# Norm powers on ScalarE and the causal mask before the exponential in a one-core hybrid decoder layer

## The chip, the cores and the metric

The kernel runs on one core of a Trainium2 chip, in one launch. The metric is the device time in microseconds. The median of three runs is 2675.95 us (2674.31 to 2677.8). Engine names are those of the profile: PE is TensorE, PEld its weight loads, DVE is VectorE, ACT is ScalarE, POOL is GpSimd and SP is SyncE.

## The reference

One layer over 512 tokens of width 2048, in float32. The parts that the change touches are the norms of queries and keys and the attention without softmax:

```python
proj = rmsnorm(x, attn_norm_g[i]) @ w_in[i]       # u, v_sgu, q, k, v_att, g_a, g_b
q = rmsnorm(q.reshape(B, S, SB_HEADS, SB_HEAD_DIM), q_norm_g[i])   # 8 heads of 128
k = rmsnorm(k.reshape(B, S, SB_HEADS, SB_HEAD_DIM), k_norm_g[i])
# for each block of 128 queries:
z = jnp.einsum('bhqd,bhkd->bhqk', qi, kf) * scale
strict = key_pos[None, :] < q_pos[:, None]
log_beta = jax.nn.log_sigmoid(z)
log_1m = jnp.where(strict, jax.nn.log_sigmoid(-z), 0)
tail = lax.cumsum(log_1m, axis=3, reverse=True) - log_1m
w = jnp.where(strict, jnp.exp(log_beta + tail), 0)
out = jnp.einsum('bhqk,bhkd->bhqd', w, vf)
```

Around it stand a gated chunk mixing of 8 groups (`y_a`), `x += (sigmoid(g_a) * (y_a @ w_up_a) + sigmoid(g_b) * (y_b @ w_up_b)) @ w_o`, a SwiGLU of hidden width 5632, and a last gate `x += sigmoid(rmsnorm(x) @ w_pg) * (p @ w_ple)`.

## The kernel before

All tensors are held transposed: features on the 128 partitions, the 512 tokens along the free dimension. Each float32 operand is split into a high part, rounded by ScalarE (`whi`, `parts`), and a low remainder, formed by VectorE (`wlo`). Most products are Strassen products on 2 x 2 blocks (lines 284 to 286 and 695), with the sums mixed on VectorE and ScalarE (lines 718 to 799).

Weights come in units through `Weights`: SyncE loads the blocks (L329, L331), GpSimd issues one more load that adds onto what has landed (L351), ScalarE rounds (L347), VectorE sums (L363) and subtracts (L344). Units are prepared a few ahead (`prepare_early`, `prepare_late`) with three slots.

The order is made while the program is laid out. The projections run in four rounds: q, k and v for two heads each, then three or four gate projections. TensorE's stream is the sequence of weight units. After each unit or part of one, `tick` advances a counter and lets the waiting side steps run; such a step is a generator started with `beside`, which says by `yield n` after how many ticks it goes on. The side steps of a round are `q_prep`, `k_prep`, `v_prep` and `attention`, so their small matmuls stand among the large ones of the next projections. A scheduler orders each engine's instructions within these bounds, and each engine works through its queue in that order.

In `q_prep` and `k_prep` a head is transposed into a PSUM bank of the two-buffer tag `small` (`flip`, L1032). `token_rms` squares and sums it on ScalarE (L1039), adds a scaled epsilon on VectorE (L1047) and raises to the power -0.5 on GpSimd (L1049). For q VectorE multiplies by 128^-0.5 (L1064). ScalarE scales the transposed q by the result (`times`, L1054), and the same line scales v by the first norm. k's result scales the logits later (L1109, L1110).

`attention` runs over 2 heads x 4 key blocks = 8 blocks a round, 32 in all, each in four steps. `stage_a` makes logits and log(1 + exp(-|z|)) on ScalarE. `stage_m` forms two tensors on VectorE: `w`, the log of beta (L1116), and `s`, the negated log of 1 - beta (L1118); GpSimd masks `s` (L1120), copies a row (L1127) and clears row 0 (L1128). `stage_b` and `stage_c` split `s` (L1131, L1135). `stage_d` sums `s` over keys with a triangular matmul (L1141, L1142), subtracts it from `w` on VectorE (L1146), takes the exponential on ScalarE (L1147) and masks on GpSimd (L1148). `stage_m` of the next block is laid out in the tick before `stage_d` of the present one. `finish` multiplies the four `w` with v (L1157).

Operands of later products are `Form` objects. Those with spilled inputs stand in the list `builds`; `tick` fetches the block of one that has none (`fetch`) and later starts its steps. `plain` is called by a product that needs a form's plain half at once and advances its steps there; if the form has no block, its first step loads one itself (`raw`).

Of the kernel before, what the change touches and what calls it, by code (L numbers as in the profile page):

```python
# [12 lines left out]
F32 = mybir.dt.float32  # L13
F32R = mybir.dt.float32r
AF = mybir.ActivationFunctionType
ALU = mybir.AluOpType
# [3 lines left out]
P = 128  # L20
T = 512
NT = T // P
# [5 lines left out]
GROUPS = 8  # L28
PLE = 256
EPS = 1e-6  # L30

OUT = "SSSSPPPP"
PASSES = "SSSSSSSS", "SSSSSSSS", "SSSSPP"
# [34 lines left out]
def hybrid_layer(  # L68
# [18 lines left out]
    nc = tc.nc  # L87

    consts = ctx.enter_context(tc.tile_pool(name="consts", bufs=1))
# [99 lines left out]
    builds, seconds = deque(), deque()  # L189
# [243 lines left out]
    class Form(Staged):  # L433
# [36 lines left out]
        def plain(self):  # L470

            if self.kind == "P":
                return self.get()
            while not self.at_plain:
                self.advance()
            self.go_on()
            return self.halves(self.operand())
# [422 lines left out]
    def load_x():  # L900
# [18 lines left out]
                            fill=0.0, base=0, channel_multiplier=1)  # L919
# [3 lines left out]
    expo = consts.tile([P, 8], F32, name="expo")  # L923
# [67 lines left out]
    norm1 = Norm()  # L991
# [32 lines left out]
        return att[tag].f(start, start + n)  # L1024

    eps_cols = consts.tile([P, NT], F32, name="eps_cols")

    def flip(o):

# [10 lines left out]
                                 accum_out=ms[:, t : t + 1])  # L1040
        return ms

    def token_rms(ps, r):

        norm1.row()
        ms = squares(ps)
        nc.vector.scalar_tensor_tensor(out=ms, in0=ms, scalar=1.0 / P, in1=eps_cols,  # L1047
                                       op0=ALU.mult, op1=ALU.add)
        nc.gpsimd.tensor_tensor(out=r, in0=ms, in1=expo[:, :NT], op=ALU.pow)  # L1049

    def times(dst, ps, r):
        for t in range(NT):
# [3 lines left out]
    def q_prep(o, i):  # L1056


        for h in range(2):
            yield 2  # L1060
            ps = flip(o[:, h * T : (h + 1) * T])
            q, r = take(T), rms_tile()[:, :NT]
            token_rms(ps, r)
            nc.vector.tensor_scalar(out=r, in0=r, scalar1=float(P) ** -0.5, scalar2=None,  # L1064
                                    op0=ALU.mult)
            yield 1
            times(q.f(), ps, r)
            yield 2
            if not h:
                y_b[i] = take(1024)  # L1070
            nc.scalar.activation(y_b[i].f(h * T, (h + 1) * T), flip(q.f()), AF.Copy,
                                 scale=gcol[:, g_q : g_q + 1])
            give(q)
# [12 lines left out]
    def attention(rnd, kT, rk, v):  # L1086
        state = {}
        yield 1
        qT = y_b[rnd].f()
        zh, zl = (att[t].own() for t in ("zh", "zl"))  # L1090

        def sums(j):
            return a_tile("zs", (NT - j) * P, j % 2 * T)

        def weights(h, j):
            return a_tile(f"w{j}", (NT - j) * P, (j == NT - 1) * h * P)

        def first(j):

            return (sums(j) if j == NT - 1 else a_tile("first", (NT - j) * P, (j == 1) * 2 * P))[0:1]  # L1100

        def stage_a(h, j):
            n = (NT - j) * P
            r = rk[:, 4 * h + j : 4 * h + j + 1]
            z = small_bank()[:, :n]
            c = h * T + j * P
            nc.tensor.matmul(z, kT[:, c : c + P], qT[:, c : (h + 1) * T], start=True, stop=True)  # L1107
            l, s = a_tile("l")[:, :n], sums(j)
            nc.scalar.activation(l, z, AF.Abs, scale=r)  # L1109
            nc.scalar.activation(s, z, AF.Copy, scale=r)  # L1110
            nc.scalar.activation(l, l, AF.Exp, scale=-1.0)
            nc.scalar.activation(l, l, AF.Ln, bias=1.0)

        def stage_m(h, j):
            l, s, w = a_tile("l")[:, : (NT - j) * P], sums(j), weights(h, j)
            nc.vector.scalar_tensor_tensor(out=w, in0=s, scalar=0.0, in1=l,  # L1116
                                           op0=ALU.min, op1=ALU.subtract)
            nc.vector.scalar_tensor_tensor(out=s, in0=s, scalar=0.0, in1=l,  # L1118
                                           op0=ALU.max, op1=ALU.add)
            nc.gpsimd.affine_select(out=s[:, :P], in_=s[:, :P], pattern=[[1, P]],  # L1120
                                    compare_op=ALU.is_gt, fill=0.0, base=0,
                                    channel_multiplier=-1)


            if j < NT - 1:
                if j:
                    nc.gpsimd.tensor_copy(first(j), s[0:1])  # L1127
                nc.gpsimd.memset(s[0:1, :P], 0.0)  # L1128

        def stage_b(j):  # L1130
            nc.scalar.activation(zh[:, : (NT - j) * P], sums(j), AF.Copy)  # L1131

        def stage_c(j):
            n = (NT - j) * P
            in_turn(nc.vector.tensor_tensor(out=zl[:, :n], in0=sums(j), in1=att["zh"].f(0, n),  # L1135
                                            op=ALU.subtract))

        def stage_d(h, j):
            n, w = (NT - j) * P, weights(h, j)
            tp, t = small_bank()[:, :n], tris[j < NT - 1]  # L1140
            nc.tensor.matmul(tp, t, zh[:, :n], start=True, stop=False)  # L1141
            nc.tensor.matmul(tp, t, zl[:, :n], start=False, stop=True)  # L1142
            if j:
                nc.vector.tensor_tensor(out=sums(j - 1)[0:1, P:], in0=tp[0:1], in1=first(j),
                                        op=ALU.add)
            nc.vector.tensor_tensor(out=w, in0=w, in1=tp, op=ALU.subtract)  # L1146
            nc.scalar.activation(w, w, AF.Exp)  # L1147
            nc.gpsimd.affine_select(out=w[:, :P], in_=w[:, :P], pattern=[[1, P]],  # L1148
                                    compare_op=ALU.is_gt, fill=0.0, base=0,
                                    channel_multiplier=-1)  # L1150
            state[h, "w", j] = w

        def finish(h):
            y = small_bank()
            for j in range(NT):
                c = h * T + j * P
                nc.tensor.matmul(y[:, j * P :], v[:, c : c + P], state.pop((h, "w", j)),  # L1157
                                 start=j == 0, stop=j == NT - 1)
            nc.scalar.activation(qT[:, h * T : (h + 1) * T], y, AF.Copy)
            if h == 1:  # L1160
                nc.sync.dma_start(out=y_spill[rnd], in_=qT)
                give(y_b[rnd])
                y_done["b", rnd] = True

        blocks = [(h, j) for h in range(2) for j in range(NT - 1, -1, -1)]
        stage_a(*blocks[0])
        yield 1
        stage_m(*blocks[0])
        yield 1
        stage_a(*blocks[1])  # L1170
        for i, (h, j) in enumerate(blocks):
            ahead = blocks[i + 1 : i + 3]
            stage_b(j)
            yield 1
            if i == NT:
                finish(0)
            stage_c(j)
            if ahead:
                stage_m(*ahead[0])
            yield 1  # L1180
            stage_d(h, j)
            if ahead[1:]:
                stage_a(*ahead[1])
            yield 1
        yield 1
        finish(1)
        if rnd == 3:
            for tag in ("first", "k", "v", "zs", "zh", "zl"):
                give(att.pop(tag))
# [109 lines left out]
    for n, ((w, i), pr) in enumerate(zip(order, made())):  # L1299
        if n == 0:  # L1300
            row1 = norm1.row()
            nc.vector.tensor_scalar(out=eps_cols, in0=norm1.mean, scalar1=EPS, scalar2=None,
                                    op0=ALU.mult)
        if n == 0:
            a_tiles()
        o = pr.out(block(w, i) if n < 3 else None)
        if w == "q":
            beside(q_prep(o, i))
        elif w == "k":
            kT, rk = o, rms_tile()  # L1310
            beside(k_prep(kT, rk))
            beside(attention(i, kT, rk, a_tile("v", 1024)), 6)
        elif w == "v":
            beside(v_prep(o, a_tile("v", 1024)))
        elif w == "s":
            scaled(o, row1)
            nc.scalar.activation(o, o, AF.Gelu_apprx_tanh)
            beside(sgu_v(i, o))
        elif w == "u":
            scaled(o, row1)  # L1320
            nc.scalar.activation(o, o, AF.Gelu_apprx_tanh)
            nc.vector.tensor_tensor(out=y_a[i].f(), in0=o, in1=y_a[i].f(), op=ALU.mult)
            y_done["a", i] = True
        else:
            d = tc.dram_tile([P, 1024], F32, name=nm("gsp"))
            nc.sync.dma_start(out=d, in_=o)
            gate_spill[w, i] = d
# [96 lines left out]
    for c, units in enumerate(hs):  # L1424
# [3 lines left out]
        for j in range(KU):  # L1428
# [8 lines left out]
            if not end:  # L1437
                after(2, lambda o=o, j=j: nc.gpsimd.dma_start(
                    out=spill["x1", j], in_=o, accum_op=ALU.add))
# [123 lines left out]
```

## Time and profile before

| | |
|---|---|
| median of three runs | 2675.95 us (2674.31 to 2677.8) |
| the profiled execution | 2676.21 us |
| its span, first to last instruction | 2674.5 us |
| granted TensorE clock, mean | 0.999 |
| the four attention rounds lie at | about 100 to 600 us |

The profile is of one execution. A row of a group gives line, engine, operation, shapes and count, then busy time and mean duration in ns, then the idle time just before these instructions and what ended it. A row of the waits gives who waited for whom, the total in us, how often, and the longest. In the timeline the first two numbers are start and duration in us.

### The profile page before, as it was taken

Reading aid. Unit: us, or ns where it says so; the run is one execution under the profiler, and the core shown is the slowest. Engines: PE = TensorE matmul, PEld = TensorE weight load, DVE = VectorE, ACT = ScalarE, POOL = GpSimd, SP = SyncE. Lnnn points to the kernel's source line nnn. Section 1 sums busy time; section 2 is a strip of 40 time slices with the busy share of each in tenths; the row PEclk is TensorE's granted clock in tenths of the full one; section 3 lists DMA queues with packets and bytes.
Section 4 is the critical chain, followed back from the end, with each engine's and each line's share of the span. In section 5 each row is a group of like instructions: output and inputs, shape, how many; then the busy total and the mean of one; then the engine's idle time right before and its main releaser. Section 6 shows DMA issues by size and latency. Waiting matters only on the chain.

```text
span 2674.5 us, 42586 instructions
## 1 busy us (share of the span) xinstructions
PE 2647.8 (99%) x15496; PEld 2322.1 (87%) x15496; DVE 2206.1 (82%) x3720; ACT 1392.0 (52%) x2171; POOL 471.2 (18%) x565
## 2 busy tenths in 40 slices
PE   8999999999999999999999999999999999999999
PEld 7889898988998889988888888888888888889898
DVE  8587878787887666678888888888889989989776
ACT  7656565665554334365444444444445445445543
POOL 0232323232220000001111111111111211211010
PEclk9999999999999999999999999999999999999999
DMA  7577777777776457668888888888788989978784
GB/s 230 151 186 175 180 173 184 173 179 201 178 187 199 141 154 210 188 213 195 220 217 206 207 202 201 204 202 206 195 208 226 263 219 272 226 238 257 242 241 132
DMA packets 285939, 540.25 MB, mean 202 GB/s; under 512 B 25632, under 2 KB 138016, under 8 KB 285728
## 3 DMA queue, kind: packets, MB, share of 16 engines
q1 hardware_dynamic: 224624, 424.25, 49.0%
q0 software_dynamic: 61104, 113.27, 27.0%
q8 instruction: 121, 1.98, 0.3%
q14 instruction: 90, 0.74, 0.1%
HBM read 490.24 MB, written 47.19 MB: 201 GB/s over the span
## 4 chain that ended last, share of the span: by engine, by line
PE 89%; DVE 5%; ACT 2%; DMA 2%; issue 1%; POOL 1%; SPq 0%; DVEq 0%; ACTq 0%; POOLq 0%
PE ps L695 48%; PE ps L286 11%; PE ps L285 11%; PE ps L284 11%; PE small L695 6%; DVE wlo L344 1%; DVE out L754 1%; PE small L1157 1%; DMA wholes<-x 1%; PE small L1032 1%; DVE wholes L363 1%; ACT whi L347 1%; DVE parts L275 0%; PE small L1107 0%; POOL wholes L1120 0%
## 5 line engine op out<-in xcount | busy, mean ns | idle before, releaser
L695 PE MATMUL ps<-parts,whi 128*128 128x512 f32 x3960 | 1324.8, 397 | 0.3 <-DVE p L754 0.3
L347 ACT ACTIVATE whi<-wholes 128x512 fp32r<-128x512 f32 (+3 forms) x933 | 866.5, 942 | 785.1 <-DVE wholes L363 270.9
L344 DVE TENSOR_TENSOR wlo<-wholes,whi 128x512 fp32r<-128x512 f32 (+3 forms) x933 | 974.4, 1078 | 82.5 <-ACT whi L347 82.1
L695 PEld LDWEIGHTS ps<-parts,wlo 128*128 128x128 f32 x3960 | 743.7, 188 | 167.8 <-issue 1.0
L695 PE MATMUL ps<-parts,wlo 128*128 128x256 f32 x3960 | 784.3, 279 | 0.1
L285 PE MATMUL ps<-parts,whi 128*128 128x256 f32 (+1 forms) x2070 | 678.3, 328 | 1.0 <-DVE parts L275 0.9
L286 PE MATMUL ps<-parts,wlo 128*128 128x256 f32 (+1 forms) x2070 | 677.9, 328 | 1.1 <-DVE wlo L344 1.1
L284 PE MATMUL ps<-parts,whi 128*128 128x256 f32 (+1 forms) x2048 | 668.0, 328 | 8.2 <-ACT parts L274 5.9
L695 PEld LDWEIGHTS ps<-parts,whi 128*128 128x128 f32 x3960 | 637.7, 189 | 6.1 <-issue 1.0
L285 PEld LDWEIGHTS ps<-parts,whi 128*128 128x128 f32 x2070 | 392.5, 190 | 41.4 <-DVE parts L275 2.5
L284 PEld LDWEIGHTS ps<-parts,whi 128*128 128x128 f32 x2048 | 388.2, 190 | 44.0 <-ACT parts L274 7.4
L286 PEld LDWEIGHTS ps<-parts,wlo 128*128 128x128 f32 x2070 | 392.8, 190 | 35.5 <-DVE wlo L344 2.3
L363 DVE TENSOR_TENSOR wholes<-wholes 128x256 f32<-128x256 f32 (+1 forms) x806 | 338.7, 420 | 21.3 <-DVE wlo L344 3.0
L754 DVE TENSOR_TENSOR out<-out,ps 128x256 f32<-128x256 f32 x460 | 190.5, 416 | 142.1 <-ACT out L751 141.8
L351 POOL DMA_DIRECT2D wholes<-w_ffn_in x172 | 150.1, 872 | 690.0 <-DVE wholes L363 268.5
L351 POOL DMA_DIRECT2D wholes<-w_in x132 | 117.8, 894 | 480.6 <-DVE wholes L363 125.9
L695 PE MATMUL small<-parts,whi 128*128 128x512 f32 x440 | 174.5, 397 | 0.0
L275 DVE TENSOR_TENSOR parts<-wholes,parts 128x1024 fp32r<-128x1024 f32 (+4 forms) x138 | 131.5, 965 | 18.9 <-ACT parts L274 18.9
L274 ACT ACTIVATE parts<-wholes 128x1024 fp32r<-128x1024 f32 (+4 forms) x138 | 113.2, 845 | 44.8 <-DVE wholes L513 25.7
L351 POOL DMA_DIRECT2D wholes<-w_ffn_out x64 | 55.9, 873 | 355.2 <-DMA wholes<-w_ffn_out 87.6
L751 ACT ACTIVATE out<-ps 128x256 f32<-128x256 f32 x243 | 91.0, 384 | 46.6 <-PE ps L695 43.3
L1403 ACT ACTIVATE out<-out 128x512 f32<-128x512 f32 x44 | 27.9, 633 | 159.6 <-DVE out L1402 159.6
(120 smaller groups left out, 1735.5 us busy)
## 6 DMA issues: line engine op xcount, KB each, us to landing
wholes<-w_ffn_in SPq DMA_DIRECT2D x172, 384.0 KB, 5.7
wholes<-w_in SPq DMA_DIRECT2D x132, 384.0 KB, 4.8
wholes<-w_ffn_in SPq DMA_DIRECT2D x172, 256.0 KB, 4.9
wholes<-w_ffn_in POOLq DMA_DIRECT2D x172, 256.0 KB, 5.4
wholes<-w_in SPq DMA_DIRECT2D x132, 256.0 KB, 4.1
wholes<-w_in POOLq DMA_DIRECT2D x132, 256.0 KB, 4.9
wholes<-w_ffn_out SPq DMA_DIRECT2D x64, 384.0 KB, 6.2
wholes<-hid SPq DMA_DIRECT2D x42, 512.0 KB, 6.1
```

What stands on the lines that cost most here:

```text
L274: return (nc.scalar.activation(hi, src, AF.Copy), nc.vector.tensor_tensor(out=lo, in0=src, in1=hi.bitcast(F32), op=ALU.subtract))
L275: nc.vector.tensor_tensor(out=lo, in0=src, in1=hi.bitcast(F32), op=ALU.subtract))
L284: nc.tensor.matmul(ps, sh, mh, start=start, stop=False)
L285: nc.tensor.matmul(ps, sh, ml, start=False, stop=False)
L286: return nc.tensor.matmul(ps, sl, mh, start=False, stop=stop)
L344: in_turn(nc.vector.tensor_tensor(out=self.lo[:, blocks], in0=r, in1=h.bitcast(F32), op=ALU.subtract))
L347: in_turn(nc.scalar.activation(h, r, AF.Copy))
L351: nc.gpsimd.dma_start(out=raw[:, 3:5], in_=self.src[:, 1:3], accum_op=ALU.add)
L363: in_turn(nc.vector.tensor_tensor(out=o, in0=x, in1=y, op=ALU.add))
L695: m = nc.tensor.matmul(out, l, r, start=first and k == 0, stop=last and k == 1)
L751: in_turn(nc.scalar.activation(out, x, AF.Copy, scale=scale))
L754: in_turn(nc.vector.tensor_tensor(out=out, in0=x, in1=y, op=op))
```

## The change

`token_rms` takes a scale and an epsilon tile, and its power becomes two ScalarE activations, Ln and then Exp with scale -0.5. For q it is called with scale 1 and an epsilon times 128, so that the factor 128^-0.5 is in the result and the VectorE rescaling goes. The mask on `w` moves from `stage_d`, after the exponential with fill 0, to the end of `stage_m`, ahead of it, with fill -10000. `plain` takes a form out of `builds` before it advances its steps.

```diff
+MASKED = -1e4
...
             if self.kind == "P":
                 return self.get()
+            if not self.at_plain and self in builds:
+                builds.remove(self)
             while not self.at_plain:
                 self.advance()
...
+    eps_q = consts.tile([P, NT], F32, name="eps_q")
...
-    def token_rms(ps, r):
+    def token_rms(ps, r, scale=1.0 / P, eps=eps_cols):
 
         norm1.row()
         ms = squares(ps)
-        nc.vector.scalar_tensor_tensor(out=ms, in0=ms, scalar=1.0 / P, in1=eps_cols,
+        nc.vector.scalar_tensor_tensor(out=ms, in0=ms, scalar=scale, in1=eps,
                                        op0=ALU.mult, op1=ALU.add)
-        nc.gpsimd.tensor_tensor(out=r, in0=ms, in1=expo[:, :NT], op=ALU.pow)
+        nc.scalar.activation(ms, ms, AF.Ln)
+        nc.scalar.activation(r, ms, AF.Exp, scale=-0.5)
...
             q, r = take(T), rms_tile()[:, :NT]
-            token_rms(ps, r)
-            nc.vector.tensor_scalar(out=r, in0=r, scalar1=float(P) ** -0.5, scalar2=None,
-                                    op0=ALU.mult)
+            token_rms(ps, r, 1.0, eps_q)
...
                 nc.gpsimd.memset(s[0:1, :P], 0.0)
+            nc.gpsimd.affine_select(out=w[:, :P], in_=w[:, :P], pattern=[[1, P]],
+                                    compare_op=ALU.is_gt, fill=MASKED, base=0,
+                                    channel_multiplier=-1)
...
             nc.scalar.activation(w, w, AF.Exp)
-            nc.gpsimd.affine_select(out=w[:, :P], in_=w[:, :P], pattern=[[1, P]],
-                                    compare_op=ALU.is_gt, fill=0.0, base=0,
-                                    channel_multiplier=-1)
...
-            nc.vector.tensor_scalar(out=eps_cols, in0=norm1.mean, scalar1=EPS, scalar2=None,
-                                    op0=ALU.mult)
+            for eps, c in ((eps_cols, EPS), (eps_q, EPS * P)):
+                nc.vector.tensor_scalar(out=eps, in0=norm1.mean, scalar1=c, scalar2=None,
+                                        op0=ALU.mult)
```

## The prediction

> **What bounds the kernel now.** I read the page first: busy time by engine and the chain that ended last.
>
> ```profile
> span 2674.5 us, 42586 instructions
> ...
> PE 2647.8 (99%) x15496; PEld 2322.1 (87%) x15496; DVE 2206.1 (82%) x3720; ACT 1392.0 (52%) x2171; POOL 471.2 (18%) x565
> ...
> PE 89%; DVE 5%; ACT 2%; DMA 2%; issue 1%; POOL 1%; SPq 0%; DVEq 0%; ACTq 0%; POOLq 0%
> ```
>
> TensorE has work in 2647.8 of 2674.5 us, so all its idle time is 26.7 us, 1.0%. The edit neither adds nor removes a matmul. It can pay only where it takes away a wait of TensorE (or a low clock), and it can cost only by making new ones. So the second view is who TensorE waited for (total us, times, longest).
>
> ```profile
> PE small L1142 <- DVE parts L1135: 3.5, 4, 0.9
> PE small L1032 <- ACT wholes L1054: 2.2, 1, 2.2
> PE small L1157 <- POOL wholes L1148: 2.2, 4, 0.6
> ...
> PE small L1214 <- ACT wholes L1054: 1.3, 1, 1.3
> ...
> PE small L1107 <- ACT wholes L1054: 0.7, 3, 0.2
> ```
>
> The list names the places. L1148 is the mask after the exponential, which moves: 2.2 us, four times, once per round. The 2.2 us at L1032 is a transpose waiting for L1054, the scaling by the norms' powers, in round 0. L1214 is the gating branch, whose power (L931) stays on GpSimd; the rows left out belong to the start, the weights and later stages. Third, the granted clock: read in windows of 100 us it is 1.00 everywhere but in one, so I cut that one more finely around the 2.2 us wait (time, PE, PEld, DVE, ACT, POOL busy, PEclk, DMA).
>
> ```profile
> 100.00:200.00 100.00, 95.88 (x581) 83.06 (x580) 78.58 (x148) 63.18 (x133) 35.34 (x46) 0.98 0.70 173
> ```
>
> ```profile
> 100.80:104.20 3.40, 1.06 (x8) 0.83 (x9) 2.77 (x6) 2.61 (x11) 1.64 (x2) 1.00 0.59 86
> 104.20:107.60 3.40, 3.40 (x17) 3.21 (x16) 0.33 (x1) 2.37 (x7) 1.21 (x2) 0.50 0.58 183
> ```
>
> Behind the stretch in which TensorE had 1.06 us of work in 3.40 stands one stretch of 3.40 us at clock 0.50. The wait thus had a second price: half of 3.40, 1.70 us.
>
> **Part 1: the powers of q and k go to ScalarE.** Sixteen GpSimd powers and eight VectorE rescalings go; 32 tiny ScalarE instructions (Ln, Exp on 128x4) come.
>
> ```profile
> L1039 ACT ACTIVATE sq<-small 128x128 f32<-128x128 f32 x96 | 26.5, 278 | 13.8 <-PE small L1032 11.9
> ...
> L1049 POOL TENSOR_TENSOR rr<-ms,expo 128x4 f32<-128x4 f32 x16 | 24.6, 1540 | 3.3 <-DVE ms L1047 3.3
> ...
> L1039 ACT ACTIVATION_READ_ACCUMULATOR sq<-small 128x1 f32 x96 | 19.0, 198 | 0.0
> ...
> L1064 DVE TENSOR_SCALAR rr<-rr 128x4 f32<-128x4 f32 x8 | 1.4, 170 | 12.7 <-POOL rr L1049 12.7
> ```
>
> ```profile
> 100.00:700.00 600.00, 589.72 (x3725) 522.54 (x3724) 478.36 (x872) 365.49 (x758) 182.77 (x236) 1.00 0.73 180
> ```
>
> No ScalarE instruction on 128x4 stands in the trace. Its price lies below the 278 ns of 128x128 and near the 198 ns of 128x1; I take 200 ns, 400 ns a pair, against 1540 ns for the power and 170 ns for the rescaling. ScalarE gains 32 x 0.2 = 6.4 us on 365.49 busy of 600 in the four rounds, hidden while it has that room. GpSimd loses 24.6 us, VectorE 1.4 us of work and 12.7 us of standing still. The added epsilon row is one more VectorE instruction of that 170 ns size.
>
> What this does to round 0 is read in the timeline, engines mixed (start, duration, and in brackets the idle time before).
>
> ```profile
> 96.57 0.16 DVE L1047 SCALAR_TENSOR_TENSOR ms<-ms,eps_cols 128x4 f32<-128x4 f32 x1 [1.46 <-ACT sq L1039]
> ...
> 98.07 0.67 ACT L347 ACTIVATE whi<-wholes 128x512 fp32r<-128x512 f32 x1
> ...
> 99.38 0.88 POOL L351 DMA_DIRECT2D wholes<-w_in  x1 [2.76 <-DMA wholes<-w_in]
> ...
> 99.95 1.38 POOL L1049 TENSOR_TENSOR rr<-ms,expo 128x4 f32<-128x4 f32 x1
> ...
> 100.40 0.40 PE L695 MATMUL ps<-parts,whi 128*128 128x512 f32 x1
> 101.36 0.17 DVE L1064 TENSOR_SCALAR rr<-rr 128x4 f32<-128x4 f32 x1 [4.62 <-POOL rr L1049]
> ...
> 101.56 0.37 ACT L1054 ACTIVATE wholes<-small,rr 128x128 f32<-128x128 f32 x1 [2.83 <-DVE rr L1064]
> 101.83 1.14 ACT L1054 ACTIVATE wholes<-small,cols 128x128 f32<-128x128 f32 x4
> ...
> 103.02 0.66 PE L1032 MATMUL small<-ident,wholes 128*128 128x128 f32 x4 [2.23 <-ACT wholes L1054]
> ...
> 103.80 0.80 PE L1032 MATMUL small<-ident,out 128*128 128x128 f32 x4
> ```
>
> The sum of squares was ready at 96.73, but GpSimd's queue is in order: the power sat behind L351, the issue of an accumulating weight load that waited 2.76 us for a landing. It began at 99.95. VectorE stood 4.62 us for it, ScalarE 2.83, and the value scaling (cols) queued behind on ScalarE frees the PSUM bank that TensorE needs at 100.80. In the new kernel ScalarE is free at 98.74. From there it owes two pairs of Ln and Exp (0.8) and eight scalings, about 1.15 per four (2.3): all done by 101.85, the first four by about 100.7. TensorE wants the bank at 100.80, so 0 to 1.1 us of wait is left; I take 0.5. Saved: 2.23, and 0.12 of idle between the end of that transpose group (103.68) and the next at 103.80, less 0.5: 1.85 us. With at most 1.1 us idle the low clock should go too, since the waits of 1.3 us (L1214) and less in the list are followed by no such stretch (and the 0.98 of its window is 1.7 us in 100): another 1.70 us.
>
> The added wait: ScalarE now waits for VectorE's small add (L1047) sixteen times, and behind it are queued weight splits (L347), on which the VectorE splits and TensorE depend. Cover: ScalarE already stands for VectorE 4.97 us at a time without a split coming late:
>
> ```profile
> 188.37 0.68 DVE L1146 TENSOR_TENSOR wholes<-wholes,small 128x512 f32<-128x512 f32 x1
> ...
> 189.09 0.63 ACT L1147 ACTIVATE wholes<-wholes 128x512 f32<-128x512 f32 x1 [4.97 <-DVE wholes L1146]
> ...
> 189.80 1.15 POOL L1148 TENSOR_SCALAR_AFFINE_SELECT wholes<-wholes 128x128 f32<-128x128 f32 x1 [0.21 <-ACT wholes L1147]
> ...
> 191.00 1.45 PE L1157 MATMUL small<-wholes 128*128 128x512 f32 x3 [0.54 <-POOL wholes L1148]
> ```
>
> So I cost it at nothing; with the cover gone each is worth at most its wait, some 0.5 to 1.5 us. Nor do I expect a table switch: the kernel already runs Exp and Ln together (L1111, L1112), and the first load after the start is for the GELU:
>
> ```profile
> L1317 ACT ACT_TABLE_LOAD  x1: 1283/1283/1283, 636.1 to 636.1; - x1
> ```
>
> If each pair did switch there and back, 32 x 1.28 = 41 us of ScalarE time would come, mostly in its idle time.
>
> **Part 2: the mask goes ahead of the exponential.** Still 32 selects on 128x128. In the last fence the sum's end is ScalarE's at 189.72, and TensorE was ready at 191.00 - 0.54 = 190.46; only the select, to 190.95, made it wait. Without it the weights are there 0.74 us early, so all four waits go: 2.2 us. Nothing else is late there next: the operand is the exponential's own.
>
> The new place is GpSimd's queue right behind the fill of row 0 (L1128), on data VectorE has just written, and the waiting instruction is now VectorE's subtraction (L1146), with the weight sums (L363) and splits (L344) behind it. The room is read from the tightest of round 0's blocks, in the timeline, with a source view of the select and a row of the waits behind it.
>
> ```profile
> 173.07 0.38 POOL L1128 MEMSET wholes<- 1x128 f32 x1
> ...
> 175.16 0.90 POOL L351 DMA_DIRECT2D wholes<-w_in  x1 [0.40 <-DVE wholes L363]
> ...
> 178.88 0.54 DVE L1146 TENSOR_TENSOR wholes<-wholes,small 128x384 f32<-128x384 f32 x1
> ...
> 185.45 0.68 DVE L1135 TENSOR_TENSOR parts<-wholes,parts 128x512 fp32r<-128x512 f32 x1
> ```
>
> ```profile
> L1148 POOL TENSOR_SCALAR_AFFINE_SELECT wholes<-wholes x32: 284/709/3865, 130.3 to 597.6; 128x128 f32<-128x128 f32 x32
> ```
>
> ```profile
> POOL wholes L351 <- DVE wholes L363: 123.5, 24, 21.9
> ```
>
> From 173.45 to 178.88 are 5.4 us, against a median select of 0.71 and a longest of 3.87. Cost: nothing, unless an L351 that waits longer stands in between.
>
> **Part 3: no second fetch.** The loads of the spilled rows say whether one ever happened.
>
> ```profile
> wholes<-hid SPq DMA_DIRECT2D x42, 512.0 KB, 6.1
> wholes<-x SPq DMA_DIRECT2D x37, 512.0 KB, 5.7
> ```
>
> 22 hidden blocks, of which 20 are Strassen forms read twice by design, make 42; for x: 8 and 8 of the first residual, 8 + 5 of the second for the gate, 8 for the end make 37. There is no load too many, so nothing is saved on SyncE's queue. At most a preparation step comes a tick later: 0.
>
> **The sum.** 1.70 + 1.85 + 2.2 = 5.75 us; the 0.7 at L1107 may go too, as ScalarE gets to it earlier, and is kept for the range. The profiled execution took 2676.21 us (span 2674.5, 1.71 around it), and 0.26 above the median 2675.95 of three runs. 2676.21 - 5.75 = 2670.46 for the profile, 2670.2 against the median. 0.2% here is 5.35 us, about what a measurement of this kernel can tell from no change, so the forecast lies on that edge: its own range, 5.2 (1.1 us of wait left) to 6.95 (none, and L1107 gone), is 2669.0 to 2670.8.
>
> **The rivals.** *The low clock stays* (24%). Either the rest of the wait falls together with other small gaps in one clock stretch, or it has another cause. Then 1.85 + 2.2 = 4.05 us, 2671.9; a few new waits of 0.2 to 0.9 us, such as the list has, lead to the same place. For it: one occurrence only ties wait and clock together. Against it: they stand back to back. The Trainium skill (TensorE: Matmul & The Clock Gate, HAM oscillation) gives the rule "no PE-idle gaps >~3.4µs"; the wait here is 2.23 us, so by that rule it would not have cost the clock and this rival would hold. The rows speak against the rule as a limit: 1.06 us of work in 3.40 was enough.
>
> *The select is caught behind a weight load* (20%, slower). If the scheduler puts an L351 between L1128 and the select, and that issue is released over 5.4 us later (the mean of the 24 waits for L363 is 5.1, the longest 21.9), VectorE stands at L1146 with the splits behind it. At one such wait a round, each 0.5 to 5 us for TensorE and with 1.70 of low clock when it passes about 2 us, I take 3.5: 14 us, less the 5.75 gained, is 8 slower: 2684. Against it: one L351 stands between at 175.16 (idle 0.40) and would still leave the select in time.
>
> *More goes than the list names* (10%). The waits at L1142 (3.5) come from VectorE's order in the last block; with 12.7 us less standing still on VectorE they may go as well, with L1107: 5.75 + 3.5 + 0.7 = 9.95, 2666.0. Against it: the row of L1135 at 185.45 has no bracket: VectorE was busy right before it, so the wait is its load and not a stall.
>
> **How the numbers follow.** Forecast 46%, the others 24, 20 and 10. The forecast lies over the 5.35 us in some four fifths of its range (38%) and under it in the rest (8%). Faster: 38 + 10 = 48%; same: 24 + 8 = 32%; slower: 20%. The range goes from 2665.5, just past the largest gain, to 2680, past half of the slower case, which leaves out about 14%.
>
> **What would show it.** Right: TensorE's waits hold neither L1157 nor a 2.2 us L1032; clock 1.00 from 20 us on; no L1064; Ln and Exp near 200 ns; table loads as before; 42 and 37 loads. Wrong: a new TensorE wait on ScalarE's splits near 100, 230 or 370 us (part 1's cover), VectorE's L1146 waiting for GpSimd (part 2's), or a half-clock stretch left in place.

## The result, and the profile after

| | before | after |
|---|---|---|
| median of 20 runs each, side by side | 2677.06 us (2674.29 to 2681.32) | 2672.64 us (2668.32 to 2674.92) |
| ratio after : before | | 0.9984 [0.9977, 0.9991] |
| the profiled execution | 2676.21 us | 2670.7 us |
| its span | 2674.5 us | 2669.0 us |

The new kernel is 4.4 us or 0.16% faster, 2.4 to 6.2 us by the interval. The gain is real, but it stays inside the 0.2% (5.35 us) that the prediction had set as its bound for "the same". The forecast was 5.75 us. A second set of runs of the same kernel (below) gave 0.9985.

First, the page of the kernel after: span, busy time by engine, and the chain that ended last.

```profile
span 2669.0 us, 42636 instructions
...
PE 2644.1 (99%) x15496; PEld 2320.7 (87%) x15496; DVE 2207.3 (83%) x3713; ACT 1395.7 (52%) x2203; POOL 449.1 (17%) x549
...
PE 85%; DVE 6%; DMA 3%; ACT 3%; issue 2%; POOL 1%; SPq 0%; POOLq 0%; DVEq 0%; ACTq 0%
```

TensorE has the same 15496 matmuls, with 3.7 us less busy time (2647.8 before). GpSimd has 22 us less work and ScalarE 3.7 us more. Next, the waits of TensorE in the kernel after (total us, times, longest).

```profile
PE small L1160 <- ACT wholes L1153: 2.5, 3, 0.8
PE small L947 <- DVE diag L945: 2.4, 3, 1.4
PE small L1148 <- DVE parts L1141: 2.3, 3, 1.3
...
PE small L1110 <- ACT wholes L1059: 1.3, 3, 0.5
PE small L1217 <- ACT wholes L1059: 0.9, 1, 0.9
PE small L1160 <- issue: 0.7, 1, 0.7
```

The lines have moved by 1 to 6. The 2.2 us of the transpose (L1032, now L1036) is gone, and so is the wait of `finish` (L1157, now L1160) for GpSimd. But `finish` has a new wait, for the exponential on ScalarE (L1153), 2.5 + 0.7 = 3.2 us in four places. The prediction had nothing there. The logits' wait (L1107, now L1110), 0.7 before, has grown to 1.3. The 2.4 us at L947 (L944 before, 0.3) lie in a later stage; between the profiles of this study this wait varies from under 0.2 to 3.2 us, with and without the change.

Third, the windows of round 0 (time, PE, PEld, DVE, ACT, POOL busy, PEclk, DMA) and of all four rounds.

```profile
100.80:104.20 3.40, 3.40 (x26) 3.12 (x26) 0.16 (x1) 3.40 (x12) 0.87 (x1) 1.00 0.80 200
104.20:107.60 3.40, 3.40 (x25) 3.10 (x23) 1.90 (x5) 3.40 (x13) 0.00 (x0) 1.00 0.51 83
```

```profile
100.00:700.00 600.00, 592.00 (x3764) 526.21 (x3763) 483.62 (x871) 368.17 (x781) 160.88 (x220) 1.00 0.72 181
```

Where TensorE had 1.06 us of work in 3.40 and then ran at clock 0.50, it is busy throughout at 1.00.

Fourth, the same place in the timeline of the kernel after.

```profile
95.55 0.16 DVE L1051 SCALAR_TENSOR_TENSOR ms<-ms,eps_q 128x4 f32<-128x4 f32 x1 [1.60 <-ACT sq L1043]
...
96.80 0.24 ACT L1053 ACTIVATE ms<-ms 128x4 f32<-128x4 f32 x1
...
97.14 0.24 ACT L1054 ACTIVATE rr<-ms 128x4 f32<-128x4 f32 x1
...
98.47 0.88 POOL L352 DMA_DIRECT2D wholes<-w_in  x1 [3.02 <-DVE wlo L345]
...
99.59 0.60 PE L1036 MATMUL small<-ident,wholes 128*128 128x128 f32 x4
...
100.26 0.65 PE L1036 MATMUL small<-ident,out 128*128 128x128 f32 x4
```

The norm is there at 97.38. The accumulating load (L352) still waits 3.02 us at the head of GpSimd's queue, but nothing of the norm stands behind it. Neither transpose has a bracket, so TensorE did not wait at all: the 0.5 us that the forecast kept did not come.

Fifth, the groups of the two new instructions (busy us, mean ns, idle time before them).

```profile
L1054 ACT ACTIVATE rr<-ms 128x4 f32<-128x4 f32 x16 | 3.3, 206 | 0.2
L1053 ACT ACTIVATE ms<-ms 128x4 f32<-128x4 f32 x16 | 3.3, 205 | 5.3 <-DVE ms L1051 5.2
```

They take 205 and 206 ns, estimated at 200. ScalarE stands 5.2 us for VectorE's add over sixteen times, and no new wait of TensorE for a weight split is in the list. The table load and the loads of spilled rows are as before:

```profile
L1321 ACT ACT_TABLE_LOAD  x1: 1283/1283/1283, 629.6 to 629.6; - x1
```

```profile
wholes<-hid SPq DMA_DIRECT2D x42, 512.0 KB, 6.0
wholes<-x SPq DMA_DIRECT2D x37, 512.0 KB, 6.0
```

Last, the new wait, in the timeline of the kernel after: the first `finish` of round 0.

```profile
148.16 0.67 DVE L1152 TENSOR_TENSOR wholes<-wholes,small 128x512 f32<-128x512 f32 x1
...
148.66 0.31 ACT L1137 ACTIVATE parts<-wholes 128x128 fp32r<-128x128 f32 x1 [1.00 <-POOL wholes L1123]
...
148.88 0.40 ACT L1115 ACTIVATE wholes<-wholes 128x256 f32<-128x256 f32 x1
...
149.19 1.25 ACT L348 ACTIVATE whi<-wholes 128x1280 fp32r<-128x1280 f32 x1
...
150.35 0.61 ACT L1153 ACTIVATE wholes<-wholes 128x512 f32<-128x512 f32 x1
...
151.06 1.74 PE L1160 MATMUL small<-wholes 128*128 128x512 f32 x4 [0.75 <-issue]
```

The exponential's input was complete at 148.83, but it ran at 150.35. ScalarE had stood 1.00 us for the select on `s` (L1123, L1120 before). From there the split of `s` (L1137), a step of the next block (L1115), a 1.25 us weight split (L348) and the exponential follow one another without a gap. TensorE, in order as well, stood 0.75 us at the weighted sum. Why the select on `s` was late is told in the part on why the prediction was right.

### The profile page after: what moved, and what is told of

It is laid out like the page before. It is cut to its first block, busy times and chain, and to the rows that moved or that the text cites. A ratio compares the mean times of both kernels' runs of the same rounds, so it can differ in the third digit from the quotient of the medians.

```text
span 2669.0 us, 42636 instructions
## 1 busy us (share of the span) xinstructions
PE 2644.1 (99%) x15496; PEld 2320.7 (87%) x15496; DVE 2207.3 (83%) x3713; ACT 1395.7 (52%) x2203; POOL 449.1 (17%) x549
## 4 chain that ended last, share of the span: by engine, by line
PE 85%; DVE 6%; DMA 3%; ACT 3%; issue 2%; POOL 1%; SPq 0%; POOLq 0%; DVEq 0%; ACTq 0%
PE ps L698 46%; PE ps L286 11%; PE ps L287 11%; PE ps L285 10%; PE small L698 6%; DVE wlo L345 2%; DVE out L757 1%; DMA wholes<-w_in 1%; DMA wholes<-x 1%; PE small L1160 1%; ACT whi L348 1%; PE small L1036 1%; DVE wholes L364 1%; DVE wholes L516 0%; DVE parts L276 0%
## 5 line engine op out<-in xcount | busy, mean ns | idle before, releaser
L348 ACT ACTIVATE whi<-wholes 128x512 fp32r<-128x512 f32 (+3 forms) x933 | 867.2, 942 | 774.3 <-DVE wholes L364 266.1
L345 DVE TENSOR_TENSOR wlo<-wholes,whi 128x512 fp32r<-128x512 f32 (+3 forms) x933 | 976.1, 1079 | 83.1 <-ACT whi L348 82.4
L352 POOL DMA_DIRECT2D wholes<-w_ffn_in x172 | 149.7, 870 | 688.8 <-DVE wholes L364 221.3
L352 POOL DMA_DIRECT2D wholes<-w_in x132 | 115.9, 879 | 522.6 <-DMA wholes<-w_in 132.6
L352 POOL DMA_DIRECT2D wholes<-w_ffn_out x64 | 55.8, 871 | 357.8 <-DVE wholes L516 67.6
```

The source lines that it names most:

```text
L345: in_turn(nc.vector.tensor_tensor(out=self.lo[:, blocks], in0=r, in1=h.bitcast(F32), op=ALU.subtract))
L348: in_turn(nc.scalar.activation(h, r, AF.Copy))
L352: nc.gpsimd.dma_start(out=raw[:, 3:5], in_=self.src[:, 1:3], accum_op=ALU.add)
```

## The experiments

To say where time goes, I numbered the large matmuls of each trace (those into the `ps` banks, the same in every kernel here) and took the start of the k-th. The wait of round 0 lies between numbers 400 and 425, at 99.9 and 108.9 us before; number 3200, at 605.2 us, lies behind the last `finish` of round 3. The table gives the start against that of the kernel before, in us; it is worked out from the traces and no view of the profile.

| kernel | no. 400 | no. 425 | difference: round 0's wait | no. 3200 (605.2 us) | from 425 to 3200: rest of the rounds |
|---|---|---|---|---|---|
| after | -1.04 | -5.29 | **-4.25** | -6.45 | -1.16 |
| after_again | +1.24 | -3.01 | **-4.25** | -3.35 | -0.35 |
| e1_powers | +1.22 | -3.03 | **-4.25** | -2.89 | +0.14 |
| e3_one_power | -0.84 | -5.03 | **-4.19** | -3.87 | +1.15 |
| e2_mask | -0.57 | -0.78 | **-0.21** | -2.04 | -1.26 |
| e9_power_first | -0.46 | -0.34 | **+0.12** | +0.17 | +0.52 |
| e10_power_first | +1.28 | -3.01 | **-4.29** | -1.02 | +1.99 |
| e10_again | +1.09 | -3.20 | **-4.29** | -2.05 | +1.15 |
| e5_finish_later | +0.33 | -3.92 | **-4.25** | -9.47 | -5.55 |
| e7_finish_and_m_later | -0.08 | -4.33 | **-4.25** | -0.02 | +4.31 |
| e11_own_w2 | +1.20 | -3.04 | **-4.24** | -8.38 | -5.34 |
| e11_again | -0.21 | -4.45 | **-4.24** | -9.80 | -5.35 |

The column of no. 400 is the start-up, and it differs by 2.3 us between two profiles of one and the same kernel (the first two rows). Behind no. 3200 the profiles move by another -1.5 to +8.4 us against that of the kernel before; the +8.4 is e11_own_w2, which has three stretches at clock 0.50 there. So a profile's total doesn't settle a question of 2 us; a difference at one place does.

**Either half alone.** The theory: the powers and the mask give their parts independently, the powers at round 0's wait.

*e1_powers*, the change with the mask left where it was:

```diff
-            nc.gpsimd.affine_select(out=w[:, :P], in_=w[:, :P], ..., fill=MASKED, ...)
...
             nc.scalar.activation(w, w, AF.Exp)
+            nc.gpsimd.affine_select(out=w[:, :P], in_=w[:, :P], ..., fill=0.0, ...)
```

> Only the powers of q and k go to ScalarE; the mask stays behind the exponential. Theory A (the gain is one wait in round 0): the transpose wait of 2.2 us near 100 us and the half-clock stretch behind it go, the four waits of about 0.55 us at the second finish stay: 4 to 5 us less than the kernel before. Theory B (the prediction's sum, powers 3.55 and mask 2.2): 3.5 us less, and the mask alone gives the other 2.2. Theory C (relief of GpSimd and VectorE in all rounds): 5 us or more less, with fewer waits of TensorE in rounds 1 to 3 too.

Measured: 2675.43 against 2678.34 us, 0.9986 [0.9977, 0.9995]. The waits of TensorE in e1_powers (its L1145 is the triangular matmul, L1160 `finish`, L1151 the select):

```profile
PE small L1145 <- DVE parts L1138: 3.8, 4, 1.1
PE small L1160 <- POOL wholes L1151: 2.2, 4, 0.5
```

The transpose is gone from the list; the 2.2 us of the mask is as it was. The triangular matmul's wait (3.5 before) did not shrink, although VectorE no longer stands for the powers.

*e2_mask*, the kernel before with the mask alone moved:

```diff
+            nc.gpsimd.affine_select(out=w[:, :P], in_=w[:, :P], ..., fill=-1e4, ...)
...
             nc.scalar.activation(w, w, AF.Exp)
-            nc.gpsimd.affine_select(out=w[:, :P], in_=w[:, :P], ..., fill=0.0, ...)
```

> Only the mask goes ahead of the exponential; the powers stay on GpSimd. Theory A: the 2.2 us wait near 100 us and the half-clock stretch stay, the four waits at the second finish go (2.2 us), but four waits of about 0.8 us for the exponential at the first finish come: within 1.5 us of the kernel before. Theory B: 2.2 us less, no wait at the first finish. Theory C: 1 to 2 us less.

Measured: 2678.36 against 2678.34 us, 0.9997 [0.9988, 1.0005]. Its waits of TensorE (L1157 is `finish`, L1150 the exponential, L1145 the triangular matmul):

```profile
PE small L1157 <- ACT wholes L1150: 2.5, 3, 0.9
PE small L1032 <- ACT wholes L1054: 2.5, 1, 2.5
...
PE small L1145 <- DVE parts L1138: 1.2, 2, 0.6
...
PE small L1157 <- issue: 0.8, 1, 0.8
```

The mask alone brings what it brings in the whole change: the four waits for GpSimd go, 3.3 us of new ones come at `finish`, and the triangular matmul's wait falls from 3.5 to 1.2. Net in the rounds: 1.3 us by the table, too little for the times to tell from nothing. The two halves multiply to 0.9983, the whole measured 0.9984: within the intervals of the runs they don't interact.

**One power of sixteen.** If all of the powers' gain is round 0's wait, the first is enough; if it is spread over the rounds or comes from GpSimd's lighter load, it is not. *e3_one_power*: the kernel before, with only the first power of round 0 on ScalarE.

```diff
+        if on_act:                  # i == 0 and h == 0
+            nc.scalar.activation(ms, ms, AF.Ln)
+            nc.scalar.activation(r, ms, AF.Exp, scale=-0.5)
+            return
         nc.gpsimd.tensor_tensor(out=r, in0=ms, in1=expo[:, :NT], op=ALU.pow)
```

> A single one of the sixteen powers goes to ScalarE, that of round 0's first q head; all else is as before. Theory A: this one power holds the whole gain of the powers, 4 us less than the kernel before (2.35 of wait and 1.70 of half clock), the same as with all sixteen moved. Theory C: a sixteenth of it, under 0.5 us less.

Measured: 2674.18 against 2678.34 us, 0.9982 [0.9973, 0.9990]; 4.19 us at round 0's wait. The other fifteen powers on ScalarE give nothing that can be measured.

**The power's price, or its place in the queue?** The prediction blamed the load issue ahead of the power. Then a power on GpSimd is as good, if it is put ahead of that issue; if its 1.54 us against 0.41 is what matters, it is not (1.54 is the power's mean, 0.41 that of Ln and Exp together). *e9_power_first*: the kernel before, with one load made to come after the first power.

```diff
+        p = nc.gpsimd.tensor_tensor(out=r, in0=ms, in1=expo[:, :NT], op=ALU.pow)
+        if not powers:
+            powers.append(p)
+            tc.add_manual_dep(added[-1].ins, p.ins.name, ...)   # the load behind the power
```

> The kernel before with all powers on GpSimd, but the first one put ahead of the weight load issue (L351) that it had stood behind. Theory A (it is the place in GpSimd's queue that costs): the 2.2 us wait and the half-clock stretch go, 3 to 4 us less than the kernel before. Rival (a GpSimd power is too slow whatever its place): 1.5 us or more of the wait stay, under 2 us less.

Measured: 2677.99 against 2678.86 us, 0.9999 [0.9990, 1.0008]. The timeline of GpSimd shows why it says nothing on the question:

```profile
99.03 0.86 POOL L351 DMA_DIRECT2D wholes<-w_in  x1 [7.71 <-DMA wholes<-w_in]
99.59 1.36 POOL L1053 TENSOR_TENSOR rr<-ms,expo 128x4 f32<-128x4 f32 x1
100.60 1.28 POOL L351 DMA_DIRECT2D wholes<-w_in  x1
```

Another issue of L351 stood in front. It had waited 7.71 us for a landing, so the power was as late as before, and TensorE waited 2.3 us at the transpose (L1034) with clock 0.50 behind it. *e10_power_first* puts both issues behind the power (`behind` makes a load wait for it in the order):

```diff
+                    if len(powers) == 1:
+                        behind(added[-1], powers[0])     # the next load too
+                        powers.append(None)
```

> The kernel before, all powers on GpSimd, with both weight load issues (L351) of that moment put behind the first power; in e9 another one was left in front of it. Theory A (its place in GpSimd's queue costs): the power starts near 97 us instead of 100, the 2.2 us wait and the half-clock stretch go, 3 to 4 us less than the kernel before. Rival (a GpSimd power of 1.4 us and the two crossings to VectorE are too slow in any place): 1 us or more of the wait stays, under 2 us less.

The timeline of GpSimd in e10_power_first (L1061 is the power):

```profile
98.11 1.03 POOL L1061 TENSOR_TENSOR rr<-ms,expo 128x4 f32<-128x4 f32 x1 [4.83 <-DVE ms L1059]
99.11 0.91 POOL L351 DMA_DIRECT2D wholes<-w_in  x1
100.27 0.88 POOL L351 DMA_DIRECT2D wholes<-w_in  x1 [0.26 <-issue]
```

The power starts at 98.11, when its input is there. This profile is 1.28 us behind that of the kernel before at no. 400, so on that profile's clock it is 96.83 in place of 99.95. The wait and the low clock are gone with all powers still on GpSimd: 4.29 us at that place, as much as with ScalarE. So the queue was the cause, and the engine's price was not. But the time didn't follow: 2677.51 against 2678.30 us, 0.9995 [0.9986, 1.0003]. *e10_again*, the same kernel:

> The kernel of e10 once more. In its profile the wait and the half clock near 100 us were gone (4.2 us by the place of TensorE's products), in its times at most 0.14% was. Theory A: the first times were unlucky, 2 to 4 us less than the kernel before. Rival: the two loads that now stand behind the power come 3.4 and 0.9 us later and cost again what the power gains, within 1.5 us of the kernel before.

2676.38 against 2679.60 us, 0.9990 [0.9980, 1.0000]. In its windows the place is again clean (before it held 1.17 us of TensorE work in this window):

```profile
100.00:103.40 3.40, 3.40 (x25) 3.06 (x24) 2.10 (x5) 2.99 (x11) 2.10 (x2) 1.00 0.76 151
```

Some 1 to 3 us are lost again elsewhere. In the profile of e10_power_first 2.0 us come back within the rounds, in that of e10_again 1.2; but e3_one_power, whose time did follow, gives back 1.2 as well. Two loads are held behind the power, and that may cost later waits; no run isolates it, and this stays open.

**The first `finish`.** Its new wait comes from the exponential being late on ScalarE. If the weighted sum then only has to come later, laying out `finish(0)` a tick later, ahead of `stage_d` instead of ahead of `stage_c`, removes it. *e5_finish_later*:

```diff
             stage_b(j)
             yield 1
-            if i == NT:
-                finish(0)
             stage_c(j)
             if ahead:
                 stage_m(*ahead[0])
             yield 1
+            if i == NT:
+                finish(0)
             stage_d(h, j)
```

It changes part of the computation: by then `stage_m` of head 1 has overwritten head 0's weights for key block 2, and `finish(0)` reads those of head 1.

> The changed kernel with the first finish of a round (the product of weights and values of head 0) one tick later. Theory A: the four waits of about 0.8 us at the first finish (3.2 us) go, 2 to 3.2 us less than the changed kernel, so 7 us less than the kernel before. Rival: TensorE then waits at the next use of the two small PSUM banks instead, and the time stays within 1 us of the changed kernel.

Measured: 2670.49 against 2678.34 us, 0.9966 [0.9954, 0.9979]. No row of `finish` is left in its waits, and from the triangular matmul's 2.3 us only this:

```profile
PE small L1148 <- DVE parts L1141: 0.4, 1, 0.4
```

In this trace ScalarE doesn't stand for the select on `s` any more either. So the run shows that the new wait can go; it doesn't tell whether the later `finish` alone would have been enough.

Two ways to keep the reference's result. *e7_finish_and_m_later* moves that `stage_m` behind `finish(0)` as well:

```diff
-            if ahead:
+            if ahead and i != NT:
                 stage_m(*ahead[0])
             yield 1
+            if i == NT:
+                finish(0)
+                stage_m(*ahead[0])
```

> The changed kernel with the first finish of a round one tick later and the min and max step (stage_m) of the block after it moved behind it, so that the weights it reads are still there. Theory A: the four waits of 0.8 us at the first finish go as with the finish alone moved, 2 to 3.4 us less than the changed kernel. Rival: the later step makes the next split of sums late, TensorE waits there (L1148) for up to 1 us a round, and the time stays within 1 us of the changed kernel or is over it.

Measured: 2680.39 against 2678.86 us, 1.0007 [0.9998, 1.0016]. The rest of the rounds loses 4.3 us in the table. The chain `stage_m`, `stage_b`, `stage_c` now starts a tick late, and its end is what TensorE waits for, in e7's waits:

```profile
PE small L1148 <- DVE parts L1141: 6.7, 8, 1.1
...
PE small L1147 <- ACT parts L1137: 1.4, 2, 0.8
```

*e11_own_w2* gives the weights of head 1, key block 2 a tile of their own instead:

```diff
         def weights(h, j):
+            if (h, j) == (1, NT - 2):
+                if "own" not in state:
+                    state["own"] = take(2 * P, "old")
+                return state["own"].f()
             return a_tile(f"w{j}", (NT - j) * P, (j == NT - 1) * h * P)
...                                  # finish(0) a tick later, as in e5_finish_later
         finish(1)
+        give(state.pop("own"))
```

> The changed kernel with the first finish of a round one tick later, and with a block of its own for the weights that would overwrite what it still has to read. Theory A: as with the finish alone moved, the four waits of 0.8 us go and the waits at L1148 shrink: 2 to 3.5 us less than the changed kernel, 6.5 to 8 less than the kernel before. Rival: taking the block from the arena makes other blocks wait for space, and nothing is gained over the changed kernel.

Measured: 2669.95 against 2678.30 us, 0.9968 [0.9957, 0.9978]. The profile was taken of the longest run (2676.56 us, clock 0.997), with four stretches at clock 0.50. *e11_again*, the same kernel:

> The kernel of e11 once more, for a profile without the four half-clock stretches of its first one. Theory A: 6.5 to 8.5 us less than the kernel before; no wait of TensorE at the finishes, none over 0.5 us at the triangular sums. Rival: the gain was chance, 4 to 5 us less, as the changed kernel.

2669.57 against 2679.60 us, 0.9964 [0.9952, 0.9977]. Its waits hold no `finish`, and of the triangular matmul (L1152):

```profile
PE small L1152 <- DVE parts L1145: 0.7, 2, 0.5
```

This is the fastest kernel of the study, 8 to 10 us below the one before. From 425 to 3200 it gains 5.3 us, where the change alone gains 0.4 to 1.2. That agrees roughly with the new wait of 3.2 us and with the 1.6 to 2.6 us of the triangular matmul's wait (2.3 in after, 3.1 in after_again) that it takes away. Whether the kernel before gains by the same move was not tried.

**The clock, and the measurement.** *e8_stall*: the change with five ScalarE copies of 128x512 ahead of the first scaling of v, to bring the wait back without GpSimd and see whether the low clock comes with it.

```diff
+            ps = flip(o[:, h * T : (h + 1) * T])
+            if first_v:
+                first_v.pop()
+                for _ in range(5):
+                    nc.scalar.activation(v[:, :T], ps, AF.Copy)
```

> The changed kernel with five ScalarE copies of 128x512 (about 0.6 us each, of values that are overwritten) ahead of the first scaling of v, so that the same PSUM bank comes free about 3 us later, with no GpSimd in it. Theory D (the wait brings the half clock): a TensorE wait of 2 to 3 us near 100 us and a half-clock stretch of 3.4 us behind it, 4 to 5 us more than the changed kernel. Rival (the half clock had another cause): the wait alone, 2 to 3 us more, clock 1.00 throughout.

Measured: 2673.90 against 2678.86 us, 0.9984 [0.9975, 0.9993], as without the copies. The timeline of TensorE in e8_stall:

```profile
101.87 0.28 PE L287 MATMUL ps<-parts,wlo 128*128 128x256 f32 x1
102.01 0.66 PE L1036 MATMUL small<-ident,wholes 128*128 128x128 f32 x4
102.42 0.36 PE L285 MATMUL ps<-parts,whi 128*128 128x256 f32 x1
```

No wait arose. The order, made with the copies in it, has the transpose behind 411 large matmuls, where the change has it behind 404 (at 99.59 in its timeline). It tells nothing of the clock. But it fits what made the wait before: the power behind a load issue was late for reasons (a landing) that an order made beforehand did not provide for.

*after_again*, the change once more:

> The changed kernel once more, beside the three below. All theories: 4 to 5 us less than the kernel before. Theory A: no wait of over 0.3 us near 100 us, no half-clock stretch there, four waits of about 0.8 us at the first finish.

2674.45 against 2678.86 us, 0.9985 [0.9976, 0.9994].

## Why the prediction was right, and where it was not

**The powers: right, and a little larger.** The sum had 1.70 for the clock and 1.85 for the wait, 3.55 us. Measured at that place: 4.25 us in both profiles of the change and in e1_powers. The mis-sized term is the 0.5 us of wait held back for ScalarE's eight scalings: without it 1.70 + 2.35 = 4.05, and the last 0.2 is no more than the place differs by between kernels that keep the wait (-0.21 and +0.12). The working let ScalarE come to the norm only at 98.74, behind its second weight split. The new order put Ln ahead of that split: it ran at 96.80, and the first q scaling at 97.75. On the clock of the profile before, 1.04 us later, these are 97.84 and 98.79, and the last v scaling ended at 100.46, ahead of the 100.80 at which TensorE wants the bank. The cause as given, the queue of GpSimd, is shown by e10_power_first, and that one power carries it by e3_one_power. The covers held: no weight split came late, no table was switched.

**The mask: the step that failed.** "Without it the weights are there 0.74 us early, so all four waits go: 2.2 us. Nothing else is late there next", and for the new place of the select "Cost: nothing". The four waits did go. But this looked at the second `finish` of each round alone, and at VectorE's subtraction alone as what waits in the new place. At the first `finish` the new order has the weighted sum one large product earlier (behind 685, 686 before), and on ScalarE it has the split of `s` (L1137) ahead of the exponential. That split stands for the select on `s`, once in each round, in the groups of the kernel after:

```profile
L1137 ACT ACTIVATE parts<-wholes 128x128 fp32r<-128x128 f32 (+3 forms) x32 | 15.0, 467 | 15.3 <-DVE wholes L1150 6.0 <-POOL wholes L1131 4.9 <-POOL wholes L1123 4.0
```

By these rows the exponential is late by this 1.00 us, and TensorE waits 0.75 to 0.84 us, four times: 3.2 us of new waits. Against that the triangular matmul's waits fell by 0.4 (after_again) to 1.2 in the change and 2.3 in e2_mask. The net of 2.2 predicted was 0.35 to 1.16 us from product 425 to 3200 in the change's two profiles and 1.26 in e2_mask's, whose time was 0.9997.

So the forecast of 5.75 came out near the measured 4.4 by 0.7 more in one term and 1.0 to 1.9 less in the other; that the two offset is luck. The gain lies under the forecast's own range of 5.2 to 6.95, and the medians' interval (2.4 to 6.2) reaches into it. It lies nearer to the 4.05 of the first rival, whose second form, "a few new waits of 0.2 to 0.9 us", is what came.

**The place of the new select: wrong, and this is what the new waits cost.** The prediction had it "right behind the fill of row 0". The order put it ahead of the other select, the one on `s`, in the timeline of GpSimd after:

```profile
145.43 2.95 POOL L1132 TENSOR_SCALAR_AFFINE_SELECT wholes<-wholes 128x128 f32<-128x128 f32 x1 [0.70 <-DVE wholes L1119]
148.34 0.29 POOL L1123 TENSOR_SCALAR_AFFINE_SELECT wholes<-wholes 128x128 f32<-128x128 f32 x1
148.68 0.89 POOL L352 DMA_DIRECT2D wholes<-w_in  x1
```

Here the select on `s` starts when the 2.95 us of the moved one are over, and ScalarE stood 1.00 us for it. By the rows of ScalarE the exponential would have come 1.00 us earlier without that, more than any of the four waits. The same stand of four times 1.00 us is in the traces of after_again and e2_mask. In that of e1_powers, with the mask at its old place, there is neither the stand nor the wait. No run puts the moved select behind the other alone, so this is read from the traces and not shown by an experiment. The rival *the select is caught behind a weight load* did not occur: in the source view of L1132 no engine waits for it. What was late is what stood behind it.

**More goes than the list names.** It named VectorE's standing less as the reason for which the 3.5 us of the triangular matmul could go. That reason fell: with the powers alone the wait is 3.8 us. It falls with the mask's place in the order (1.2 in e2_mask, 2.3 in after, but 3.1 in after_again) and with the later `finish` (0.4 and 0.7). The 0.7 at L1107, which the range let go, grew to 1.3 in the change and 1.2 in e2_mask.

**The low clock stays.** It did not: at that place the clock is 1.00 in every profile without the wait. The Trainium skill's limit (TensorE: Matmul & The Clock Gate, HAM oscillation: "no PE-idle gaps >~3.4µs") is no safe bound by these runs. After the first 6 us the longest wait of TensorE in any profile here is 2.5 us. Stretches at half clock followed waits of 2.23 us (before), of 1.74 us (after_again, near 24 us) and, in e1_powers, of 1.62 us. For the last, here are the timeline of TensorE and the window behind it:

```profile
23.66 0.50 PE L285 MATMUL ps<-parts,whi 128*128 128x512 f32 x1 [1.62 <-ACT whi L348]
```

```profile
25.10:28.50 3.40, 3.40 (x9) 2.63 (x8) 3.40 (x8) 1.97 (x4) 0.42 (x1) 0.50 1.00 332
```

None followed a wait of 1.86 us in e2_mask at 2519, whose next window reads 1.00:

```profile
2519.40:2522.80 3.40, 3.40 (x17) 2.91 (x18) 1.26 (x2) 1.67 (x3) 0.01 (x1) 1.00 0.64 109
```

Nor did one follow a wait of 2.47 us in e9_power_first at 2518. In e11_own_w2 two waits of only 0.82 and 0.84 us, ending at 2419.21 and 2420.55, had one behind them: the window from 2420.80 to 2424.20 reads 0.51. So waits between 1.6 and 2.5 us sometimes bring the low clock and sometimes not, and shorter ones close together did once. Round 0's wait in the kernel before is one that did in each profile taken of it, also in e2_mask and e9_power_first.

**No second fetch.** Right: 42 and 37 loads, nothing gained, nothing lost.

## What to carry to other kernels

A tiny instruction that many wait for is better placed on an engine whose queue holds nothing that waits for a transfer; look at what stands ahead of it in the queue before its own price. Where an instruction leaves the path, look at every place where its result is used, not at the one with the wait: the order is made anew without it, and the next late thing is met (here 3.2 us of new waits for 2.2 removed). Where an instruction is moved into another place of a queue, look at what then stands behind it and not only at who waits for its result. A gain of 0.16% is settled by the same place in several profiles, not by totals, whose start-up alone differed by 2.3 us.

## What was not expected of the hardware

A wait of 1.62 us of TensorE was followed by one stretch of about 3.4 us at clock 0.50, waits of 1.86 and 2.47 us by none. Each stretch costs about 1.7 us by an estimate (half of 3.4), as much as such a wait itself.

The same select of 128x128 on GpSimd took 0.29 us and 2.95 us within four microseconds, as the profile gives these spans. In the rounds of the kernel after, all nine selects of 1.4 us or more lie over 1.5 to 2.2 us of VectorE's weight splits (L345), and the seven during which VectorE ran nothing took 0.29 us each. The runs don't show whether the one is the cause of the other.
